# Turning float32-staged pairs of bf16 values as 32-bit words in a matmul, gelu, matmul kernel

## The chip, the cores and the metric

The kernel runs on one core of a Trainium2 chip. The core has five engines that run side by side and meet through semaphores: TensorE (PE: matmuls, and as PEld the loading of their stationary operand), VectorE (DVE), ScalarE (ACT), GpSimd (POOL) and SyncE (SP). TensorE reads SBUF and writes PSUM, which has eight banks of 128 x 512 float32. The metric is the time of one execution in microseconds (us); lower is better.

## The reference

```python
m, k, n, p = 1024, 1024, 2048, 1024      # a: m x k, b: k x n, c: n x p, all float32
h = np.matmul(a, b)
h = 0.5 * h * (1 + np.tanh(np.sqrt(2 / np.pi) * (h + 0.044715 * h ** 3)))
return np.matmul(h, c).astype(np.float32)
```

Two dense products with a gelu (its tanh form) between them.

## The kernel before

All products are made with bf16 or rounded float32 operands. The first product is made transposed: a bank of PSUM holds 128 columns of b by 512 rows of a, so the contraction index k must lie on the partitions for both. b has it there already; a, which is loaded with its rows on the partitions, must be turned. The turned a is the tile `aT`: two halves h of 512 rows each, and for each half eight slices of 128 values of k, 512 columns wide. A quarter q of a is two of these slices, 256 values of k.

The columns of b go through four stretches. The first 512 are made by plain matmuls, `mm1` (line 114), while a and b arrive: four tiles t of 128 columns, two halves h, eight slices k, 64 matmuls of 128x512. This stage is what the change edits. The next 512 columns (`zero`) and then 1024 (`one`) are made by a seven-product scheme (`seven`, its matmuls all on line 212), and so is the whole second product (`two`). The scheme needs sums and differences of quarters of its operands: `t1` to `t4` of the moving side and `s1` to `s4` of the stationary side, made by VectorE (line 170) in float32r, with two plain copies by ScalarE (lines 202 and 208). `BB` names the quarters of `aT` for `zero` and `one`. In `zero` the products run in the order P1, P2, P5, P6, P7, P4, P3; P5 needs s1 and t1, P6 needs s2 and t2, P7 needs s3 and t3, P4 needs t4, P3 needs s4.

The order of all work is written out by hand: each engine runs its instructions in the order of the program text, and semaphores make it wait where data or a buffer is not ready. PSUM banks are named: `bank(i)` gives a new tile in bank i, and the first write to it waits until the tile before it in that bank has been read.

The loads of the first stage go by two queues. From SP (lines 75 to 79) come, in float32, the pieces (0,0), (1,0) and (0,1) of a (half, quarter), and slices 0 to 2 of b's first 512 columns. From POOL (lines 85 to 104) come, converted to bf16 by the DMA, piece (1,1) of a, slice 3 of b, then for q = 2 and 3 the piece (0,q), two slices of b and the piece (1,q); then the next 512 columns of b in two loads of four slices (line 98), the rest of b, and c. A tiny copy (line 81) keeps POOL's loads behind the first piece of a.

The float32 pieces are cast by `cast_a` (VectorE line 110, ScalarE line 108) into a buffer `ab`, the slices of b by `cast_b`. `turn(h, q, i, ab)` is a generator: for each of the two slices of a quarter it emits four transposes of 128x128 bf16 (line 145) into bank i, has VectorE copy the 128x512 result into `aT` (line 146), and yields. The main program (lines 229 to 287) interleaves these steps with blocks of matmuls: `block(h, tiles, ks)` makes the matmuls of one half for some tiles and slices. For q = 1 and 2 it runs four matmuls of half 0, the four transposes of the first slice of (1,q), four matmuls, the transposes of the second slice, then three matmuls of half 1, transposes of (0,q+1), three matmuls, transposes. The fourth tile of half 1 has no bank until half 0 is finished, and is made at the end of the stage, around the turning of (1,3). `stir` emits float32 matmuls on a constant while nothing has arrived.

Of the kernel before, what the change touches and what calls it, by code (L numbers as in the profile page):

```python
# [19 lines left out]
def kernel(ctx, tc, a, b, c, out):  # L20
    nc = tc.nc
    M, K = a.shape
    _, N = b.shape
    _, P = c.shape
    H = 512
    KT = K // 128
# [3 lines left out]
    bv = b.rearrange("(kt p) n -> p kt n", p=128)  # L30
# [3 lines left out]
    consts = ctx.enter_context(tc.tile_pool(name="consts", bufs=1))  # L34
# [5 lines left out]
    def slot(tag, shape, dt, name):  # L40
        return big.tile(shape, dt, name=name, tag=tag)

    def bank(i, shape=(128, H), dt=F32, name="ps"):
        return pp.tile(list(shape), dt, name=name, tag=f"bank{i}", padded_shape=None)

    def pieces(tag, bufs, shape, dt, name):
        return small.tile(shape, dt, name=name, tag=tag, bufs=bufs)

    warm = nc.const_aps.tensor(0.0, [128, 256], F32)
    ident = consts.tile([128, 128], BF16, name="ident")  # L50
    make_identity(nc, ident)
    gate = consts.tile([128, 1], F32, name="gate")
    g = consts.tile([128, 1], F32, name="g")

    consts.tile([128, 16], F32, name="room")

    c_sb = keep.tile([128, NT, P], BF16, name="c_sb")
    hT = [keep.tile([128, NT, H], BF16, name=f"hT{h}") for h in range(2)]
    aT = slot("a", [128, 2, KT, H], BF16, "aT")
    b1 = slot("b1", [128, KT, 1024], BF16, "b1")  # L60
    b2 = slot("b2", [128, KT, 1024], BF16, "b2")


    KH = KT // 2
    stb = slot("x0", [128, KT, H], F32, "stb")
    sta = slot("x1", [128, 2, 2, 4, 256], F32, "sta")
    abq = slot("x3", [128, 4, 2, 4, 256], BF16, "abq")
# [7 lines left out]
    nc.sync.dma_start(out=sta[:, 0, 0], in_=a_part(0, 0))  # L75
    nc.sync.dma_start(out=stb[:, 0:2], in_=b_part(0))  # L76
    nc.sync.dma_start(out=sta[:, 1, 0], in_=a_part(1, 0))
    nc.sync.dma_start(out=sta[:, 0, 1], in_=a_part(0, 1))
    nc.sync.dma_start(out=stb[:, 2], in_=bv[:, 2, 0:H])

    nc.gpsimd.tensor_copy(gate, sta[:, 0, 0, 3, 0:1])
    nc.scalar.activation(g, warm[:, 0:1], AF.Gelu_apprx_tanh)


    def cast_load_a(h, q):
        nc.gpsimd.dma_start(out=abq[:, q, h], in_=a_part(h, q))

    def cast_load_b(q):
        nc.gpsimd.dma_start(out=b1[:, 2 * q:2 * q + 2, 0:H], in_=b_part(q))

    cast_load_a(1, 1)
    nc.gpsimd.dma_start(out=b1[:, 3, 0:H], in_=bv[:, 3, 0:H])
    for q in range(2, 4):
        cast_load_a(0, q)
        cast_load_b(q)
        cast_load_a(1, q)
    for k in range(0, KT, 4):
        nc.gpsimd.dma_start(out=b1[:, k:k + 4, H:], in_=bv[:, k:k + 4, ds(H, H)])
    for n in range(2):
        for k in range(0, KT, 4):  # L100
            nc.gpsimd.dma_start(out=b2[:, k:k + 4, ts(n, H)],
                                in_=bv[:, k:k + 4, ds(1024 + n * H, H)])
# [3 lines left out]
    def copy(eng, dst, src):  # L106
        if eng is nc.scalar:
            nc.scalar.activation(dst, src, AF.Copy)
        else:
            nc.vector.tensor_copy(dst, src)  # L110

    def mm1(p, t, h, ks):
        for k in ks:
            nc.tensor.matmul(p, b1[:, k, ts(t, 128)], aT[:, h, k],  # L114
                             start=(k == 0), stop=(k == KT - 1))

    def gelu(t, h, p):
# [2 lines left out]
    ps = {(0, t): bank(t) for t in range(4)}  # L120

    def stir(*widths):

        for w in widths:
            nc.tensor.matmul(ps[0, 3][:, 0:w], warm[:, 0:128], warm[:, 0:w],
                             start=True, stop=True, skip_group_check=True)

    def cast_a(h, q, *engs):

        ab = pieces("ab", 2, [128, 4, 256], BF16, "ab")  # L130
        for i, eng in enumerate(engs):
            w = 256 // len(engs)
            for j, e in enumerate(eng if isinstance(eng, tuple) else (eng,)):
                m = slice(2 * j, 2 * j + 2) if isinstance(eng, tuple) else slice(0, 4)
                copy(e, ab[:, m, ts(i, w)], sta[:, h, q][:, m, ts(i, w)])
        return ab

    def turn(h, q, i, ab):

        banks = i if isinstance(i, tuple) else (i,)  # L140
        pts = [bank(x, (128, 2, H), BF16, "pt") for x in banks]
        for n in range(2):
            pt = pts[n % len(pts)]
            for m in range(4):
                nc.tensor.transpose(pt[:, n, ts(m, 128)], ab[:, m, ts(n, 128)], ident)  # L145
            nc.vector.tensor_copy(aT[:, h, 2 * q + n], pt[:, n])  # L146
            yield

    def cast_b(k, *engs):
        c0 = 0  # L150
        for i, eng in enumerate(engs):
            w = (H - c0) if i == len(engs) - 1 else H // len(engs) // 128 * 128
            copy(eng, b1[:, k, ds(c0, w)], stb[:, k, ds(c0, w)])
            c0 += w

    def block(h, tiles, ks):
        for k in ks:
            for t in tiles:
# [57 lines left out]
    def pair(i):  # L216
        x = slot(f"x{i}", [128, 2, 4, H], F32R, "x1")
        return x[:, 0], x[:, 1]

    BB = [[aT[:, 0, 0:4], aT[:, 1, 0:4]], [aT[:, 0, 4:8], aT[:, 1, 4:8]]]  # L220
# [9 lines left out]
    tn = turn(0, 0, 4, cast_a(0, 0, nc.vector))  # L230
    next(tn)
    stir(128)
    cast_b(0, nc.vector, nc.vector, nc.scalar)
    next(tn)
    stir(64)
    cast_b(1, nc.scalar)
    ab = cast_a(1, 0, nc.vector, nc.scalar)
    block(0, range(4), (0,))
    block(0, range(2), (1,))
    for _ in turn(1, 0, (7, 6), ab):  # L240
        pass
    block(0, range(2, 4), (1,))
    ab = cast_a(0, 1, (nc.scalar, nc.vector), nc.vector)
    cast_b(2, nc.scalar, nc.scalar)
    for t in range(3):
        ps[1, t] = bank(4 + t)
    zero.t[0], zero.t[1] = pair(2)
    block(1, range(3), (0,))
    tn = turn(0, 1, 7, ab)
    next(tn)  # L250
    block(1, range(3), (1,))
    next(tn)
    zero.t1(4, 0)
    for q in range(1, 3):
        k = 2 * q
        block(0, range(4), (k,))
        tn = turn(1, q, 7, abq[:, q, 1])
        next(tn)
        block(0, range(4), (k + 1,))
# [228 lines left out]
```

## Time and profile before

| | |
|---|---|
| median of 3 runs | 117.55 us (117.53 to 117.62) |
| span of the profiled execution | 115.7 us; its own total time is not given apart from the span |
| PE busy | 111.1 us, 96% of the span |
| DVE, ACT, POOL busy | 90.0, 51.4, 17.2 us |
| granted TensorE clock | 1.00 |
| first matmul of line 114, of line 212 | 6.8 us, 24.29 us |
| HBM read, written | 20.97 MB, 4.19 MB |

The front page gives the span from the first to the last instruction, busy times and the granted clock in 40 slices. The groups give, for each line and shape, the count, the busy time in us and the mean in ns of one, then the idle time of the engine just before them and what ended it. A row of the timeline has the start in us, the time it covers, the engine, the line and operation, the tiles written and read, the shape, how many instructions were merged (x4), and in brackets the idle time before and its releaser. A matmul's duration in the trace holds its drain, which overlaps the next one, so the cost of one in a stream is the distance between starts.

### The profile page before, as it was taken

What the parts mean: (1) busy time and instruction counts of PE and PEld (TensorE: products, weight loads), DVE (VectorE), ACT (ScalarE), POOL (GpSimd) and SP (SyncE); (2) the same over time, 40 slices, a digit from 0 to 9 for tenths busy, and PEclk for the clock granted to TensorE, in tenths of its full rate; (3) what the DMA queues carried; (4) which work ended last, traced back from release to release, by engine and by line L of the source; (5) the groups of instructions that cost most, each with busy time, mean ns of one, the idle gap of its engine ahead of it and who ended that gap; (6) DMA issues with size and microseconds to landing.
All of it is one profiled execution on the core that took longest, in us unless ns stands there. A gap on an engine that the chain in (4) does not pass through costs nothing.

```text
span 115.7 us, 1461 instructions
## 1 busy us (share of the span) xinstructions
PE 111.1 (96%) x542; PEld 77.1 (67%) x542; DVE 90.0 (78%) x107; ACT 51.4 (44%) x86; POOL 17.2 (15%) x29
## 2 busy tenths in 40 slices
PE   7989999999999999999999999999999999999980
PEld 6645555546776447888885444688888888888860
DVE  0347748789999998935699999999999986954770
ACT  5053000999259997166698429500124982000000
POOL 2497755223322000000000000000000000000000
PEclk9999999999999999999999999999999999999999
DMA  2999999999999999998000000060000002014993
GB/s 69 295 381 229 200 199 205 204 208 205 206 211 209 212 213 209 212 210 168 8 0 0 6 0 0 38 235 0 0 0 0 0 4 91 1 73 176 370 363 106
DMA packets 13414, 15.94 MB, mean 138 GB/s; under 512 B 736, under 2 KB 9312, under 8 KB 13408
## 3 DMA queue, kind: packets, MB, share of 16 engines
q0 software_dynamic: 8672, 9.31, 47.6%
q1 hardware_dynamic: 4736, 6.56, 15.8%
q8 instruction: 4, 0.07, 0.3%
q14 instruction: 2, 0.02, 0.0%
HBM read 20.97 MB, written 4.19 MB: 218 GB/s over the span
## 4 chain that ended last, share of the span: by engine, by line
PE 90%; DMA 5%; SPq 1%; DVE 1%; issue 0%
PE ps L212 76%; PE ps L114 11%; DMA sta<-in_a_dram 5%; PE pt L145 3%; SPq L76 0%; DVE ab L110 0%; SPq L75 0%; DVE ot L375 0%
## 5 line engine op out<-in xcount | busy, mean ns | idle before, releaser
L212 PE MATMUL ps<-x,s 128*128 128x512 f32 x128 | 29.6, 391 | 0.0
L212 PEld LDWEIGHTS ps<-x,s 128*128 128x128 f32 x128 | 24.0, 188 | 5.1
L212 PE MATMUL ps<-x,x 128*128 128x512 f32 x96 | 22.9, 394 | 0.0
L212 PEld LDWEIGHTS ps<-x,x 128*128 128x128 f32 x96 | 18.0, 188 | 3.9
L114 PE MATMUL ps<-aT,b 128*128 128x512 bf16 x64 | 16.1, 379 | 0.2 <-DVE b L110 0.2
L298 ACT ACTIVATE v<-ps 128x512 f32<-128x512 f32 x10 | 6.0, 599 | 19.1 <-PE ps L212 19.1
L212 PE MATMUL ps<-c_sb,hT 128*128 128x512 bf16 (+1 forms) x72 | 14.2, 356 | 0.0
L212 PE MATMUL ps<-x 128*128 128x512 f32 x56 | 13.2, 392 | 0.0
L212 PEld LDWEIGHTS ps<-x 128*128 128x128 f32 x56 | 10.2, 188 | 2.6 <-ACT u L298 0.4
L118 ACT ACTIVATE hT<-ps 128x512 bf16<-128x512 f32 x14 | 7.3, 595 | 9.7 <-PE ps L114 9.7
L212 PEld LDWEIGHTS <-hT 128*128 128x128 bf16 x72 | 6.9, 98 | 7.0 <-issue 0.5
L118 ACT ACTIVATE hT<-ot 128x512 bf16<-128x512 f32 x18 | 10.4, 624 | 2.0 <-DVE ot L303 2.0
L212 PE MATMUL ps<-aT,b 128*128 128x512 bf16 x48 | 10.7, 379 | 0.0
L146 DVE COPY aT<-pt 128x512 bf16<-128x512 bf16 x16 | 6.7, 423 | 5.1 <-PE pt L145 5.1
L303 DVE TENSOR_TENSOR ot<-ps,u 128x512 f32<-128x512 f32 x10 | 6.7, 690 | 5.1 <-ACT u L298 5.1
L303 DVE TENSOR_TENSOR ot<-ps,v 128x512 f32<-128x512 f32 x10 | 6.7, 688 | 4.8 <-DMA out_dram<-ot 3.8
L170 DVE TENSOR_TENSOR x<-c_sb 128x1024 fp32r<-128x1024 bf16 x8 | 9.3, 1226 | 0.0
L114 PEld LDWEIGHTS <-b 128*128 128x128 bf16 x64 | 5.7, 98 | 4.5 <-DVE b L110 0.3
L212 PEld LDWEIGHTS <-b 128*128 128x128 bf16 x48 | 4.6, 98 | 5.7 <-issue 0.3
L104 POOL DMA_DIRECT2D c_sb<-in_c_dram x8 | 5.6, 702 | 13.1 <-DMA b<-in_b_dram 12.4
L170 DVE TENSOR_TENSOR x<-b 128x1024 fp32r<-128x1024 bf16 (+1 forms) x4 | 7.0, 1752 | 0.6 <-issue 0.6
L298 ACT ACTIVATE u<-ps 128x512 f32<-128x512 f32 x10 | 5.9, 598 | 3.4 <-PE ps L212 3.2
(44 smaller groups left out, 111.3 us busy)
## 6 DMA issues: line engine op xcount, KB each, us to landing
c_sb<-in_c_dram POOLq DMA_DIRECT2D x8, 512.0 KB, 20.0
out_dram<-ot SPq DMA_DIRECT2D x13, 256.0 KB, 2.1
b<-in_b_dram POOLq DMA_DIRECT2D x6, 512.0 KB, 15.3
sta<-in_a_dram SPq DMA_DIRECT2D x3, 512.0 KB, 6.1
abq<-in_a_dram POOLq DMA_DIRECT2D x5, 256.0 KB, 7.9
out_dram<-ot SPq DMA_DIRECT2D x6, 128.0 KB, 2.0
stb<-in_b_dram SPq DMA_DIRECT2D x1, 512.0 KB, 5.3
b<-in_b_dram POOLq DMA_DIRECT2D x2, 256.0 KB, 8.2
```

The source lines that it names most:

```text
L104: nc.gpsimd.dma_start(out=c_sb[:, t:t + 2], in_=cv[:, t:t + 2])
L114: nc.tensor.matmul(p, b1[:, k, ts(t, 128)], aT[:, h, k], start=(k == 0), stop=(k == KT - 1))
L118: nc.scalar.activation(hT[h][:, t], p, AF.Gelu_apprx_tanh)
L145: nc.tensor.transpose(pt[:, n, ts(m, 128)], ab[:, m, ts(n, 128)], ident)
L146: nc.vector.tensor_copy(aT[:, h, 2 * q + n], pt[:, n])
L170: nc.vector.tensor_tensor(out=dst[:, r], in0=x[:, r], in1=y[:, r], op=op)
L212: nc.tensor.matmul(p[:, ds(c0, w)], l[:, k, ts(j, 128)], r[:, k, ds(c0, w)], start=(start and k == 0), stop=(k == self.kt - 1), skip_group ...
L298: nc.scalar.activation(st, p, AF.Copy)
L303: nc.vector.tensor_tensor(out=ot, in0=p, in1=st, op=ADD)
```

## The change

All of a is staged in float32: the five pieces that came converted from POOL's queue now come unconverted into a second staging tile, and every piece is cast by `cast_a`. The cast writes the two slices of a quarter interleaved: value k of slice 0 and value k of slice 1 stand side by side as one 32-bit word. `turn` takes 128x128 such words as float32, so four transposes, with a float32 identity, turn a whole quarter into one bank of 128x512 words, and one copy brings them into `aT`, whose last dimension is now the pair. Matmuls and the sums read `aT` with a step of two values (the class `Turned` stands for a quarter's slices). `turn` now yields after each transpose, and `block` takes a list of such turns and puts one transpose ahead of each of its matmuls. Each cast but the first is divided by rows between ScalarE (first half) and VectorE. The loads of b's next 512 columns are four of two slices, and parts of `t1`, `t2` and `t3` are emitted later.

```diff
-    ident = consts.tile([128, 128], BF16, name="ident")
+    ident = consts.tile([128, 128], F32, name="ident")
-    aT = slot("a", [128, 2, KT, H], BF16, "aT")
+    aT = slot("a", [128, 2, KT // 2, H, 2], BF16, "aT")
-    sta = slot("x1", [128, 2, 2, 4, 256], F32, "sta")
-    abq = slot("x3", [128, 4, 2, 4, 256], BF16, "abq")
+    sta = [slot(x, [128, 2, 2, 4, 256], F32, "sta") for x in ("x1", "x3")]
...
-    def cast_load_a(h, q):
-        nc.gpsimd.dma_start(out=abq[:, q, h], in_=a_part(h, q))
+    def load_a(h, q):
+        nc.gpsimd.dma_start(out=staged(h, q), in_=a_part(h, q))
...
-    for k in range(0, KT, 4):
-        nc.gpsimd.dma_start(out=b1[:, k:k + 4, H:], in_=bv[:, k:k + 4, ds(H, H)])
+    for k in range(0, KT, 2):
+        nc.gpsimd.dma_start(out=b1[:, k:k + 2, H:], in_=bv[:, k:k + 2, ds(H, H)])
...
-            nc.tensor.matmul(p, b1[:, k, ts(t, 128)], aT[:, h, k],
+            nc.tensor.matmul(p, b1[:, k, ts(t, 128)], aT[:, h, k // 2, :, k % 2],
...
-        ab = pieces("ab", 2, [128, 4, 256], BF16, "ab")
+        ab = pieces("ab", 2, [128, 4, 128, 2], BF16, "ab")
+        w = 4 // len(engs)
         for i, eng in enumerate(engs):
-            w = 256 // len(engs)
-            for j, e in enumerate(eng if isinstance(eng, tuple) else (eng,)):
-                m = slice(2 * j, 2 * j + 2) if isinstance(eng, tuple) else slice(0, 4)
-                copy(e, ab[:, m, ts(i, w)], sta[:, h, q][:, m, ts(i, w)])
+            copy(eng, ab[:, ts(i, w)].rearrange("p m k r -> p m r k"),
+                 staged(h, q)[:, ts(i, w)].rearrange("p m (r k) -> p m r k", r=2))
         return ab
 
     def turn(h, q, i, ab):
 
-        banks = i if isinstance(i, tuple) else (i,)
-        pts = [bank(x, (128, 2, H), BF16, "pt") for x in banks]
-        for n in range(2):
-            pt = pts[n % len(pts)]
-            for m in range(4):
-                nc.tensor.transpose(pt[:, n, ts(m, 128)], ab[:, m, ts(n, 128)], ident)
-            nc.vector.tensor_copy(aT[:, h, 2 * q + n], pt[:, n])
+        pt = bank(i, (128, H), F32, "pt")
+        for m in range(4):
+            nc.tensor.transpose(pt[:, ts(m, 128)], ab[:, m].rearrange("p k r -> p (k r)").bitcast(F32), ident)
+            if m == 3:
+                nc.vector.tensor_copy(aT[:, h, q].rearrange("p m r -> p (m r)").bitcast(F32), pt)
             yield
...
-    def block(h, tiles, ks):
+    def block(h, tiles, ks, turns=()):
+        turns = iter(turns)
         for k in ks:
             for t in tiles:
+                next(turns, None)
                 mm1(ps[h, t], t, h, (k,))
+        for _ in turns:
+            pass
...
-    ab = cast_a(1, 0, nc.vector, nc.scalar)
+    ab = cast_a(1, 0, nc.scalar, nc.vector)
     block(0, range(4), (0,))
-    block(0, range(2), (1,))
-    for _ in turn(1, 0, (7, 6), ab):
-        pass
-    block(0, range(2, 4), (1,))
-    ab = cast_a(0, 1, (nc.scalar, nc.vector), nc.vector)
+    block(0, range(4), (1,), turn(1, 0, 7, ab))
+    ab = cast_a(0, 1, nc.scalar, nc.vector)
...
-    block(1, range(3), (0,))
-    tn = turn(0, 1, 7, ab)
-    next(tn)
+    block(1, range(3), (0,), turn(0, 1, 7, ab))
+    ab = cast_a(1, 1, nc.scalar, nc.vector)
     block(1, range(3), (1,))
-    next(tn)
     zero.t1(4, 0)
     for q in range(1, 3):
         k = 2 * q
-        block(0, range(4), (k,))
-        tn = turn(1, q, 7, abq[:, q, 1])
-        next(tn)
+        block(0, range(4), (k,), turn(1, q, 7, ab))
+        ab = cast_a(0, q + 1, nc.scalar, nc.vector)
         block(0, range(4), (k + 1,))
-        next(tn)
+        block(1, range(3), (k,), turn(0, q + 1, 7, ab))
+        ab = cast_a(1, q + 1, nc.scalar, nc.vector)
+        block(1, range(3), (k + 1,))
         zero.t1(4, q)
-        block(1, range(3), (k,))
-        tn = turn(0, q + 1, 7, abq[:, q + 1, 0])
-        next(tn)
-        block(1, range(3), (k + 1,))
-        next(tn)
-    zero.t1(4, 3)
     block(0, range(4), (6, 7))
-    zero.t2(2, 0)
...
-    mm1(ps[1, 3], 3, 1, range(2))
-    tn = turn(1, 3, 0, abq[:, 3, 1])
-    next(tn)
-    mm1(ps[1, 3], 3, 1, range(2, 5))
-    next(tn)
-    mm1(ps[1, 3], 3, 1, (5,))
+    tn = turn(1, 3, 0, ab)
+    for k in range(4):
+        mm1(ps[1, 3], 3, 1, (k,))
+        next(tn)
+    mm1(ps[1, 3], 3, 1, (4, 5))
+    zero.t1(4, 3)
+    zero.t2(2)
...
-    zero.t3(2, 0)
-    zero.t2(2, 1)
     block(1, range(3), (6, 7))
...
         elif n == "P2":
-            zero.t3(2, 1)
+            zero.t3(2)
```

More of the change, by code (lines that the diff above doesn't have):

```diff
@@ L53 @@
     g = consts.tile([128, 1], F32, name="g")
-    consts.tile([128, 16], F32, name="room")
+    consts.tile([128, 80], F32, name="room")
     c_sb = keep.tile([128, NT, P], BF16, name="c_sb")
     hT = [keep.tile([128, NT, H], BF16, name=f"hT{h}") for h in range(2)]
-    aT = slot("a", [128, 2, KT, H], BF16, "aT")
+    aT = slot("a", [128, 2, KT // 2, H, 2], BF16, "aT")
     b1 = slot("b1", [128, KT, 1024], BF16, "b1")
@@ L73, in b_part, with staged @@
         return bv[:, 2 * q:2 * q + 2, 0:H]
-    nc.sync.dma_start(out=sta[:, 0, 0], in_=a_part(0, 0))
+    def staged(h, q):
+        return sta[q // 2][:, h, q % 2]
+    nc.sync.dma_start(out=staged(0, 0), in_=a_part(0, 0))
     nc.sync.dma_start(out=stb[:, 0:2], in_=b_part(0))
-    nc.sync.dma_start(out=sta[:, 1, 0], in_=a_part(1, 0))
-    nc.sync.dma_start(out=sta[:, 0, 1], in_=a_part(0, 1))
+    nc.sync.dma_start(out=staged(1, 0), in_=a_part(1, 0))
+    nc.sync.dma_start(out=staged(0, 1), in_=a_part(0, 1))
     nc.sync.dma_start(out=stb[:, 2], in_=bv[:, 2, 0:H])
-    nc.gpsimd.tensor_copy(gate, sta[:, 0, 0, 3, 0:1])
+    nc.gpsimd.tensor_copy(gate, staged(0, 0)[:, 3, 0:1])
     nc.scalar.activation(g, warm[:, 0:1], AF.Gelu_apprx_tanh)
-    def cast_load_a(h, q):
-        nc.gpsimd.dma_start(out=abq[:, q, h], in_=a_part(h, q))
+    def load_a(h, q):
+        nc.gpsimd.dma_start(out=staged(h, q), in_=a_part(h, q))
     def cast_load_b(q):
         nc.gpsimd.dma_start(out=b1[:, 2 * q:2 * q + 2, 0:H], in_=b_part(q))
-    cast_load_a(1, 1)
+    load_a(1, 1)
     nc.gpsimd.dma_start(out=b1[:, 3, 0:H], in_=bv[:, 3, 0:H])
     for q in range(2, 4):
-        cast_load_a(0, q)
+        load_a(0, q)
         cast_load_b(q)
-        cast_load_a(1, q)
-    for k in range(0, KT, 4):
-        nc.gpsimd.dma_start(out=b1[:, k:k + 4, H:], in_=bv[:, k:k + 4, ds(H, H)])
+        load_a(1, q)
+    for k in range(0, KT, 2):
+        nc.gpsimd.dma_start(out=b1[:, k:k + 2, H:], in_=bv[:, k:k + 2, ds(H, H)])
     for n in range(2):
@@ L218, in pair, with __init__, __getitem__ @@
         return x[:, 0], x[:, 1]
-    BB = [[aT[:, 0, 0:4], aT[:, 1, 0:4]], [aT[:, 0, 4:8], aT[:, 1, 4:8]]]
+    class Turned:
+        def __init__(self, h, k0):
+            self.h, self.k0 = h, k0
+        def __getitem__(self, at):
+            k = at[1]
+            if isinstance(k, slice):
+                k0, n = self.k0 + k.start, k.stop - k.start
+                q, r = divmod(k0, 2)
+                return aT[:, self.h, q, :, r:r + n].rearrange("p m r -> p r m")
+            q, r = divmod(self.k0 + k, 2)
+            return aT[:, self.h, q, at[2] if len(at) > 2 else slice(0, H), r]
+    BB = [[Turned(0, 0), Turned(1, 0)], [Turned(0, 4), Turned(1, 4)]]
     def quarters(b, c0, w):
@@ L229 @@
     stir(256, 256, 256, 256, 256)
-    tn = turn(0, 0, 4, cast_a(0, 0, nc.vector))
-    next(tn)
-    stir(128)
+    ab = cast_a(0, 0, nc.vector)
+    for n, _ in enumerate(turn(0, 0, 4, ab)):
+        if n == 3:
+            stir(256, 128)
     cast_b(0, nc.vector, nc.vector, nc.scalar)
-    next(tn)
-    stir(64)
     cast_b(1, nc.scalar)
-    ab = cast_a(1, 0, nc.vector, nc.scalar)
+    ab = cast_a(1, 0, nc.scalar, nc.vector)
     block(0, range(4), (0,))
-    block(0, range(2), (1,))
-    for _ in turn(1, 0, (7, 6), ab):
-        pass
-    block(0, range(2, 4), (1,))
-    ab = cast_a(0, 1, (nc.scalar, nc.vector), nc.vector)
+    block(0, range(4), (1,), turn(1, 0, 7, ab))
+    ab = cast_a(0, 1, nc.scalar, nc.vector)
     cast_b(2, nc.scalar, nc.scalar)
@@ L272 @@
     ps[1, 3] = bank(7)
-    mm1(ps[1, 3], 3, 1, range(2))
-    tn = turn(1, 3, 0, abq[:, 3, 1])
-    next(tn)
-    mm1(ps[1, 3], 3, 1, range(2, 5))
-    next(tn)
-    mm1(ps[1, 3], 3, 1, (5,))
+    tn = turn(1, 3, 0, ab)
[5 more added lines that the diff above has]
+    zero.t2(2)
     zero.t[2], x11 = pair(1)
```

## The prediction

> **What bounds the kernel now.** I read the front page first (busy shares, granted clock, the chain that ended last), then the groups kept apart by shape, for prices, then the timeline from 4 to 37 us, where the changed code runs.
>
> ```profile
> span 115.7 us, 1461 instructions
> PE 111.1 (96%) x542; PEld 77.1 (67%) x542; DVE 90.0 (78%) x107; ACT 51.4 (44%) x86; POOL 17.2 (15%) x29
> ...
> PEclk9999999999999999999999999999999999999999
> ...
> PE ps L212 76%; PE ps L114 11%; DMA sta<-in_a_dram 5%; PE pt L145 3%; SPq L76 0%; DVE ab L110 0%; SPq L75 0%; DVE ot L375 0%
> ```
>
> TensorE is the bound: 90% of the chain is its matmuls, at full granted clock, from 6.8 us to the end. So the change is worth exactly what it does to the moment at which TensorE leaves the first stage (lines 114 and 145) and begins the products (line 212, 24.29 us), if nothing behind that moment moves.
>
> ```profile
> L146 DVE COPY aT<-pt 128x512 bf16<-128x512 bf16 x16 | 6.7, 423 | 5.1 <-PE pt L145 5.1
> L434 DVE COPY ot<-ps 128x512 f32<-128x512 f32 x4 | 2.7, 690 | 0.2 <-PE ps L212 0.2
> L108 ACT ACTIVATE ab<-sta 128x512 bf16<-128x512 f32 x1 | 0.6, 629 | 0.4 <-DMA sta<-in_a_dram 0.4
> ```
>
> The prices: an eviction of 512 bf16 columns takes 0.42, one of 512 words 0.69; ScalarE's half of a cast takes 0.63.
>
> ```profile
> 5.38 0.44 PE L125 MATMUL ps<-const-float32-0.0 128*128 128x128 f32 x2
> 7.90 0.43 DVE L110 CAST ab<-sta 128x512 bf16<-128x512 f32 x1 [0.67 <-DMA sta<-in_a_dram]
> 8.38 0.62 PE L145 MATMUL pt<-ident,ab 128*128 128x128 bf16 x8
> ...
> 15.88 0.26 PEld L145 LDWEIGHTS <-abq 128*128 128x128 bf16 x4 [0.28 <-DMA abq<-in_a_dram]
> 15.93 0.39 PE L145 MATMUL pt<-ident,abq 128*128 128x128 bf16 x4
> 16.15 1.03 PE L114 MATMUL ps<-aT,b 128*128 128x512 bf16 x4
> 16.35 0.42 DVE L146 COPY aT<-pt 128x512 bf16<-128x512 bf16 x1 [0.66 <-PE pt L145]
> ...
> 19.07 2.32 PE L114 MATMUL ps<-aT,b 128*128 128x512 bf16 x10
> 21.23 0.39 PE L145 MATMUL pt<-ident,abq 128*128 128x128 bf16 x4
> ...
> 24.29 3.62 PE L212 MATMUL ps<-aT,b 128*128 128x512 bf16 x16
> ...
> 30.53 2.36 DVE L170 TENSOR_TENSOR x<-x,aT 128x1024 fp32r<-128x1024 f32 x2
> 31.42 5.75 PE L212 MATMUL ps<-x 128*128 128x512 f32 x24
> ```
>
> Three things are to be seen. A matmul takes 0.216 (ten from 19.07 to 21.23), a transpose 0.056 (four from 15.93 to 16.15). A copy starts 0.25 after the last transpose of its group starts (16.10 to 16.35), and TensorE follows VectorE by 0.05 (8.33 to 8.38). And the loads of a are nearly in the way already: the piece (half 1, quarter 2) lands at about 15.85, and its transposes start at 15.93.
>
> **The change, part by part.** I write (h,q) for a half and quarter of a, T0 to T3 for its four transposes.
>
> Removed: 32 of 64 transposes, 32 x 0.056 = 1.8 of TensorE; on VectorE 16 copies of 0.42 become 8 of 0.69, 6.7 to 5.5, beside other work. So much is gained.
>
> Added, casts: (1,1), (0,2), (1,2), (0,3), (1,3) were cast by their DMA. Now each costs ScalarE 0.63 and VectorE 0.43 after the landing. ScalarE was idle there for 9.65 us ahead of the first gelu, VectorE has per quarter 2 x 0.69 + 2 x 0.43 + 0.68 = 2.9 of some 3.9 us; the throughput is covered, the latency is not. They write 2-byte values at 4-byte steps, which no row shows: between nothing and the next larger row (ScalarE 128x1024 1.05, so +0.42). I take nothing, the same number of elements.
>
> Added, one handover per four transposes: both slices come free together, and all sit in bank 7. The next turn's T0 and the next matmuls that read the pair wait for T3 + 0.25 + 0.69 + 0.05 = 1.0. Behind a waiting T0 everything on TensorE waits. Before, a half of the work was handed over after 0.25 + 0.42 + 0.05 = 0.72, under three or four matmuls (0.65 or 0.86).
>
> The loads: a now comes unconverted on POOL's queue. The two float32 pieces from SP land 1.43 apart (7.88, 9.31), the converted (1,2) and (0,3) 1.34 apart. I charge 0.07 a piece, 0.2 by the third; bounds nothing and 0.3. The other loads of b1 go in four issues instead of two, 1.5 more of POOL's time; POOL's issues there wait for landings of loads far ahead, so that costs nothing.
>
> The price of a 32-bit transpose: no row has one. Lower bound 0.056. Upper bound: an ordinary float32 matmul of 128 columns, which is two records, 0.44 for both with the tail; four bf16 transposes take 0.39 with a tail and 0.22 without, so 0.27 and some weight loading, say 0.3. I take 0.06, since the moving identity has as many columns as before and each weight load now hides under a 0.216 matmul. The Trainium skill's page "TensorE: Matmul & The Clock Gate" (Terms, xbus) says of its transpose mode that it is four times faster for FP32; against the 0.3 that is an estimate of 0.08 and a sum of about 119.5, which no run here shows yet.
>
> The matmuls on aT now read every second bf16. Lower bound: nothing. Upper: the 24 matmuls with 4-byte operands from 31.42 to 37.01 take 0.233 each, 0.017 more. I take nothing, because part of their excess is waits for ScalarE. The Trainium skill's page "SBUF — State Buffer" (Door 1) speaks for nothing: reads stay at full rate while at least two fall into a 16-byte line, and here four would, 119.3 against 120.7 by the row. No run here shows it yet.
>
> Now the path. (1,0): T0 waits for ScalarE's half, 7.90 + 0.63 + 0.05 = 8.58 (8.38 before, and two matmuls that ran ahead of it are now behind it). Each T with its matmul takes 0.272, so T3 9.40, ready 10.40; only one matmul is between, 0.7 idle. (0,1): T3 11.22, ready 12.22, three matmuls end 11.93, 0.3 idle. (1,1): T3 13.04, ready 14.04, five matmuls end 14.18, no wait. (0,2): T3 15.00, ready 16.00. (1,2): 15.85 + 0.2 for the load, + 0.02 + 0.63 + 0.05 = 16.75: this cast decides, not what went before. From there 36 matmuls 7.78, 12 transposes 0.67, a wait of 1.0 - 0.70 = 0.30 ahead of (0; 6,7), and one of 1.0 - 0.49 = 0.51 ahead of (1; 6,7), since only two matmuls follow T3 of (1,3). Products begin at 26.01, 1.72 later.
>
> Behind it: VectorE cannot begin its subtractions until the copy of (1,3) is done (E), because the last quarter of t1 and both parts of t2 are now queued after it, and the whole of t3 after s2. At the 1.14 pitch of these rows t4 ends at E + 11.1; TensorE begins the products at E + 1.78 and needs t4's second half 9.5 later, at E + 11.25. Covered by 0.1 (0.44 before for the whole of t4); without that cover up to 0.3. The other half of b1 lands at 25.7, ahead of s1. After that TensorE has had no idle time in which a delay could vanish.
>
> Sum: +1.7, so the profile's span goes from 115.7 to 117.4. The execution's own time is its span and what lies around it; its total is not given apart, and the median of the three runs, 117.55, is 1.85 above the span; I keep that and forecast 119.3.
>
> **Rivals.**
> - The 32-bit transpose takes twice the time (0.11). Then (0,2) is ready at 16.84 and decides; 16.84 + 7.78 + 1.32 + 0.80 = 26.74, so 120.0. For it: a 4-byte weight load takes 188 ns here against 98.
> - Strided matmuls pay 0.017: 36 on this path and 48 in the products, 84 x 0.017 = 1.4, so 120.7. For it: all 4-byte rows of line 212 are slower than 0.216. Against it: they differ in the weights, too.
> - The casts slow down with their step: +0.42 at (1,2), 119.7.
> - The change doesn't do what it says, and 32-bit words pass as ordinary float32 matmuls, 0.3 each: T3 of (1,0) at 10.13, (0,2) ready at 19.9, products at 32.1, so 125.3. For it: the constant float32 matmuls do split into two records.
> - The other side: TensorE goes on past a transpose that waits. The waits that I count are 0.9 ahead of 8.58, 0.7, 0.3, 1.0 ahead of 16.75, 0.3 and 0.5, 3.7 in all; once more than 1.7 of them is filled the kernel isn't slower, and with all filled it takes 115.6. Against it: before, the matmuls that stood behind the waiting transposes of (1,0) had their operands by 7.5, and they started only at 8.84, after them.
>
> **How the numbers follow.** My forecast 0.53; doubled transpose 0.13; strided matmuls 0.11; slow casts 0.08; ordinary float32 0.07; the other side 0.05; waits that come out shorter than I count, down to no change, 0.03. The forecast alone spans 119.0 (loads land as before) to 119.6 (the wait at t4 appears). Range 118.5 to 120.9: it takes in the first four cases and leaves out 0.15. Within 0.2% (0.24 us, about what a measurement of this kernel can tell) counts as the same: faster 0.05, same 0.03, slower 0.92.
>
> **What would show it.** In the profile of the changed kernel: transposes 510 instead of 542 records on PE in all (542 if each splits in two); the copy at line 146's place 8 times at about 690; PE idle before a transpose, ended by ScalarE's cast near 8.6 and near 16.7, and by VectorE's copy near 10.4 and 12.2; the first line-212 matmul near 26.0; line-114 matmuls still 0.216 apart. If the products begin at 24.3 or sooner, the waits were wrong; if they begin at 26 and the end is not 1.7 later, the products' stage was.

## The result and the profile after

The changed kernel takes 121.59 us (median of 4 runs, 121.50 to 122.18) against 117.54 (117.39 to 117.62) for the kernel before, run beside it: ratio 1.0358, 95% interval 1.0335 to 1.0382. The forecast was slower, at 119.3 with a range of 118.5 to 120.9. The sign held, the size did not: +4.05 instead of +1.7. The profiled execution took 121.5 in all, its span is 119.7; before it was 115.7. So the 1.8 around the span is what it was, and all of the loss is inside.

From the front page of the changed kernel (busy engines, granted clock, the chain that ended last, the groups with count, busy us, mean ns, then the idle time before and its releaser):

```profile
span 119.7 us, 1412 instructions
...
PE 112.9 (94%) x505; PEld 77.8 (65%) x510; DVE 90.7 (76%) x103; ACT 55.4 (46%) x91; POOL 18.7 (16%) x31
...
PEclk9999999999999999999999999999999999999999
...
PE ps L215 74%; PE ps L116 9%; DMA sta<-in_a_dram 5%; PE pt L143 3%; DVE aT L145 3%; ACT ab L110 1%; SPq L78 0%; SPq L77 0%; DVE ot L378 0%
...
L116 PE MATMUL ps<-aT,b 128*128 128x512 bf16 x62 | 18.0, 388 | 1.1 <-DVE b L112 0.5
...
L145 DVE COPY aT<-pt 128x512 f32<-128x512 f32 x8 | 5.5, 692 | 9.7 <-PE pt L143 9.7
...
L143 PE MATMUL pt<-ident,ab 128*128 128x128 f32 x32 | 8.6, 287 | 1.4 <-DVE aT L145 1.1
...
L110 ACT ACTIVATE ab<-sta 128x512 bf16<-128x512 f32 x7 | 5.5, 780 | 6.9 <-DMA sta<-in_a_dram 5.1
```

The clock is full throughout, so it explains nothing. There are 32 transposes (510 weight loads; five matmul records are missing from this trace) and eight copies of 0.69, as forecast. New in the chain are VectorE's copy (3%, 3.6 us) and ScalarE's cast (1%): TensorE now waits for them. And three prices are not those of the prediction: ScalarE's half of a cast takes 0.78 (0.63 before), a matmul on `aT` 388 ns (379 before, drain included), and the transposes, which only the spacing shows. The timeline of the same kernel (start, time covered, engine, line, tiles, shape, count; in brackets the idle time and its releaser):

```profile
8.70 0.33 PE L143 MATMUL pt<-ident,ab 128*128 128x128 f32 x1 [0.35 <-ACT ab L110]
...
9.43 0.27 PE L143 MATMUL pt<-ident,ab 128*128 128x128 f32 x1
...
9.54 0.39 PE L116 MATMUL ps<-aT,b 128*128 128x512 bf16 x1
...
9.76 0.27 PE L143 MATMUL pt<-ident,ab 128*128 128x128 f32 x1
...
10.07 0.69 DVE L145 COPY aT<-pt 128x512 f32<-128x512 f32 x1 [1.74 <-PE pt L143]
...
10.88 0.14 PEld L143 LDWEIGHTS pt<-ident,ab 128*128 128x128 f32 x1 [1.02 <-ACT b L110]
10.91 0.30 PE L143 MATMUL pt<-ident,ab 128*128 128x128 f32 x1 [0.65 <-DVE aT L145]
...
13.09 0.30 PE L143 MATMUL pt<-ident,ab 128*128 128x128 f32 x1 [0.20 <-DVE aT L145]
...
17.52 0.30 PE L143 MATMUL pt<-ident,ab 128*128 128x128 f32 x1 [0.20 <-DVE aT L145]
...
25.95 1.97 PE L116 MATMUL ps<-aT,b 128*128 128x512 bf16 x8 [0.33 <-DVE aT L145]
27.76 3.78 PE L215 MATMUL ps<-aT,b 128*128 128x512 bf16 x16
```

Read it by starts. A transpose holds TensorE for 9.54 - 9.43 = 0.11 (0.109 to the nanosecond in the trace), not 0.06; the matmul after it for 9.76 - 9.54 = 0.22 (0.226). The copy starts 0.31 after its last transpose and runs 0.69, and TensorE follows at 10.91, 0.15 later: 1.15 from hand to hand. The products begin at 27.76 instead of 24.29: 3.46 of the 4.07 us of span is lost by there. Another 0.60 is lost behind it, 0.48 of it because 48 matmuls on `aT` in the products are 0.010 farther apart, too.

### The profile page after: what moved, and what is told of

Read it like the earlier page. It is cut to its first block, busy times and chain, and to the rows that moved or that the text cites. A ratio compares the mean times of both kernels' runs of the same rounds, so it can differ in the third digit from the quotient of the medians.

```text
span 119.7 us, 1412 instructions
## 1 busy us (share of the span) xinstructions
PE 112.9 (94%) x505; PEld 77.8 (65%) x510; DVE 90.7 (76%) x103; ACT 55.4 (46%) x91; POOL 18.7 (16%) x31
## 4 chain that ended last, share of the span: by engine, by line
PE 86%; DMA 5%; DVE 3%; issue 1%; SPq 1%; ACT 1%
PE ps L215 74%; PE ps L116 9%; DMA sta<-in_a_dram 5%; PE pt L143 3%; DVE aT L145 3%; ACT ab L110 1%; SPq L78 0%; SPq L77 0%; DVE ot L378 0%
## 5 line engine op out<-in xcount | busy, mean ns | idle before, releaser
L116 PE MATMUL ps<-aT,b 128*128 128x512 bf16 x62 | 18.0, 388 | 1.1 <-DVE b L112 0.5
L145 DVE COPY aT<-pt 128x512 f32<-128x512 f32 x8 | 5.5, 692 | 9.7 <-PE pt L143 9.7
L215 PE MATMUL ps<-aT,b 128*128 128x512 bf16 x47 | 11.1, 387 | 0.1
L116 PEld LDWEIGHTS <-b 128*128 128x128 bf16 x64 | 6.3, 98 | 7.0 <-issue 1.0
L143 PE MATMUL pt<-ident,ab 128*128 128x128 f32 x32 | 8.6, 287 | 1.4 <-DVE aT L145 1.1
L110 ACT ACTIVATE ab<-sta 128x512 bf16<-128x512 f32 x7 | 5.5, 780 | 6.9 <-DMA sta<-in_a_dram 5.1
L215 PEld LDWEIGHTS <-b 128*128 128x128 bf16 x48 | 4.5, 96 | 6.3 <-issue 0.3
L112 DVE CAST ab<-sta 128x512 bf16<-128x512 f32 (+1 forms) x8 | 4.1, 511 | 4.9 <-DMA sta<-in_a_dram 4.9
```

Of the source, the lines that this page charges most:

```text
L116: nc.tensor.matmul(p, b1[:, k, ts(t, 128)], aT[:, h, k // 2, :, k % 2], start=(k == 0), stop=(k == KT - 1))
L143: nc.tensor.transpose(pt[:, ts(m, 128)], ab[:, m].rearrange("p k r -> p (k r)").bitcast(F32), ident)
L145: nc.vector.tensor_copy(aT[:, h, q].rearrange("p m r -> p (m r)").bitcast(F32), pt)
L215: nc.tensor.matmul(p[:, ds(c0, w)], l[:, k, ts(j, 128)], r[:, k, ds(c0, w)], start=(start and k == 0), stop=(k == self.kt - 1), skip_group ...
```

## Experiments

Every kernel ran beside the kernel before on its chip. The table has medians and the difference between the two; the changed kernel itself stands at +4.05. "First product" is the start of the first matmul of the products in the profiled execution. Names that begin with b start from the kernel before, those with a from the changed one. The two with one time have no interval.

| run | us | before | difference | ratio (95% interval) | first product |
|---|---|---|---|---|---|
| before | 117.54 | | | | 24.29 |
| after | 121.59 | 117.54 | +4.05 | 1.0358 (1.0335 to 1.0382) | 27.76 |
| b_step2_products | 118.02 | 117.49 | +0.53 | 1.0056 (1.0029 to 1.0083) | 24.36 |
| a_dense_reads | 120.83 | 117.49 | +3.34 | 1.0295 (1.0268 to 1.0322) | 28.04 |
| a_f32r_turn | 120.32 | 117.49 | +2.83 | one time | 26.58 |
| b_float_staging | 118.13 | 117.49 | +0.64 | 1.0052 (1.0037 to 1.0067) | 24.77 |
| a_copy_twice | 126.41 | 117.60 | +8.81 | one time | 32.69 |
| a_two_ahead | 119.91 | 117.60 | +2.31 | 1.0196 (1.0172 to 1.0220) | 25.94 |
| a_vector_first | 121.19 | 117.60 | +3.59 | 1.0305 (1.0285 to 1.0325) | 27.55 |
| a_dense_cast | 121.30 | 117.60 | +3.70 | 1.0313 (1.0293 to 1.0333) | 27.50 |
| a_four_undone | 119.12 | 117.53 | +1.59 | 1.0129 (1.0089 to 1.0169) | 25.66 |
| a_turn_later | 118.72 | 117.54 | +1.18 | 1.0073 (1.0039 to 1.0107) | 25.24 |
| b_three_first | 117.71 | 117.53 | +0.18 | 1.0011 (0.9987 to 1.0036) | 24.53 |
| b_three_split | 117.69 | 117.53 | +0.16 | 1.0004 (0.9988 to 1.0021) | 24.74 |

**Does the step of two values slow a matmul?** First in the kernel before, where nothing else changes:

```diff
+            turned = any(r is x for row in BB for x in row)
...
-                nc.tensor.matmul(p[:, ds(c0, w)], l[:, k, ts(j, 128)], r[:, k, ds(c0, w)],
+                rk = r[:, k, ds(c0, w)]
+                if turned:
+                    rk = r[:, k // 2 * 2:k // 2 * 2 + 2].rearrange("p r m -> p (r m)").rearrange("p (m s) -> p m s", s=2)[:, :, k % 2]
+                nc.tensor.matmul(p[:, ds(c0, w)], l[:, k, ts(j, 128)], rk,
```

> The kernel before, with one thing of the change alone: the 48 bf16 matmuls of zero and one that read aT take every second value out of two neighbouring slices instead of 512 values in a row (so these products see mixed slices; the amount of work is the same). Theory 'step': reading with a step of two costs 0.010 a matmul, 226 ns from start to start where they were 216, 48 x 0.010 = 0.49, so 118.0 (117.9 to 118.1). Rival 'company': the 226 ns seen after the change come from something else beside them; then they stay at 216 ns and the time at 117.5.

The groups of this kernel, the stage's matmuls first, then those of the products:

```profile
L114 PE MATMUL ps<-aT,b 128*128 128x512 bf16 x64 | 16.3, 379 | 0.3 <-DVE b L110 0.3
...
L216 PE MATMUL ps<-aT,b 128*128 128x512 bf16 x48 | 11.2, 387 | 0.0
```

Same type, same shape, same weights; only the step differs, and 379 becomes 387 (216 to 226 ns from start to start). 48 x 0.010 = 0.48 of the +0.53. Then the counterpart, the changed kernel with all 112 matmuls on `aT` reading in a row:

```diff
-            nc.tensor.matmul(p, b1[:, k, ts(t, 128)], aT[:, h, k // 2, :, k % 2],
+            nc.tensor.matmul(p, b1[:, k, ts(t, 128)], aT[:, h, k // 2].rearrange("p m r -> p (m r)")[:, ds(k % 2 * H, H)],
...
-            return aT[:, self.h, q, at[2] if len(at) > 2 else slice(0, H), r]
+            return aT[:, self.h, q].rearrange("p m r -> p (m r)")[:, ds(r * H, H)]
```

> The changed kernel, whose 112 matmuls on aT read 512 values in a row of each quarter's words instead of every second one (so they see mixed slices; all else is as in the changed kernel). Theory 'step': 216 ns again; the 64 of the first stage give 0.65, of which the waits for the copies take some 0.2 back because the matmuls that cover them are shorter, the 48 of the products 0.49, together 0.95, so 120.6 (120.4 to 120.8). Rival 'company': 226 ns stay, 121.6.

The matmuls are 216 ns apart everywhere again, and the excess falls from 4.05 to 3.34, by 0.71 where 0.95 was expected. Its profiled execution (121.45, the longest of its four) can't say where the rest went by absolute times, since there piece (1,0) of a landed at 8.6 instead of 7.85. Counted from the first transpose of (1,0), it has 18.60 to the products where the changed kernel has 19.06, 0.46 less. Behind the start of the products it has 91.64 instead of 91.98, only 0.34 less where 0.49 was expected, because a wait appears there that the changed kernel does not have. At 39.00 a weight load of the products starts after 0.32 of waiting for VectorE's first addition into `ot` (line 306), which stands behind VectorE's sums in its order, and two matmuls start 0.28 and 0.34 apart instead of 0.23. That is 0.16 lost: TensorE comes sooner, VectorE does not. So 0.46 and 0.34, 0.80 in all, stand against 0.71 in the medians. The price of the step is shown; what it is worth in time depends on what else is ready.

**What does a 32-bit transpose cost, and is it the type or the word?** float32r words of the same size in place of float32 (its casts write half the elements, 128 of each 256):

```diff
+    ident_r = consts.tile([128, 128], F32R, name="ident_r")
+    nc.vector.tensor_copy(ident_r, ident)
...
-        ab = pieces("ab", 2, [128, 4, 128, 2], BF16, "ab")
+        ab = pieces("ab", 2, [128, 4, 128], F32R, "ab")
...
-            copy(eng, ab[:, ts(i, w)].rearrange("p m k r -> p m r k"),
-                 staged(h, q)[:, ts(i, w)].rearrange("p m (r k) -> p m r k", r=2))
+            copy(eng, ab[:, ts(i, w)], staged(h, q)[:, ts(i, w), 0:128])
...
-        pt = bank(i, (128, H), F32, "pt")
+        pt = bank(i, (128, H), F32R, "pt")
...
-            nc.tensor.transpose(pt[:, ts(m, 128)], ab[:, m].rearrange("p k r -> p (k r)").bitcast(F32), ident)
+            nc.tensor.transpose(pt[:, ts(m, 128)], ab[:, m], ident_r)
...
```

> The changed kernel with its transposes in float32r instead of float32. The words turned are rounded float32 values of one slice, not pairs, and each cast makes half as many elements; so only the distance from a transpose to the matmul behind it is compared, not the time. Theory 'columns': a float32 word takes TensorE two cycles per moving column, 128 x 2 at the clock of these rows is 107 ns, which is all of the 108 ns seen; a float32r one takes one, so 55 to 60 ns. Rival 'fixed': the price is that of a 4-byte weight load or of changing between 4-byte and 2-byte work, and 108 ns stay. The time would be about 119.7 by the first and 121.1 by the second.

Three neighbours in its timeline, PE alone:

```profile
9.27 0.40 PE L118 MATMUL ps<-aT,b 128*128 128x512 bf16 x1
...
9.31 0.42 PE L145 MATMUL pt<-ident_r,ab 128*128 128x128 f32 x1
...
9.57 0.40 PE L118 MATMUL ps<-aT,b 128*128 128x512 bf16 x1
```

The split between the two is modelled oddly here (0.26 and 0.04), but a pair is 9.57 - 9.27 = 0.30, against 9.76 - 9.43 = 0.33 in the changed kernel and 0.272 before. To the nanosecond the pairs take 301, 335 and 272, so with 226, 226 and 216 for the matmul a transpose takes 75 (float32r), 109 (float32) and 56 (bf16). Neither named value was met: of the 53 ns that float32 takes more than bf16, some 34 go with float32, and some 19 stay with float32r. What makes these parts is open. What matters here is that one float32 word costs as much as two bf16 values: behind the first piece 28 x 0.109 = 3.05 stand against 56 x 0.056 = 3.14, so halving the count gained nothing.

**What does staging in float32 cost by itself?** The kernel before with float32 pieces and engine casts, but bf16 transposes, so that every piece is converted as in the changed kernel and written in a row:

```diff
-    abq = slot("x3", [128, 4, 2, 4, 256], BF16, "abq")
+    sta = [slot(x, [128, 2, 2, 4, 256], F32, "sta") for x in ("x1", "x3")]
...
-        nc.gpsimd.dma_start(out=abq[:, q, h], in_=a_part(h, q))
+        nc.gpsimd.dma_start(out=staged(h, q), in_=a_part(h, q))
...
-        tn = turn(1, q, 7, abq[:, q, 1])
+        tn = turn(1, q, 7, ab)
         next(tn)
         block(0, range(4), (k + 1,))
+        ab = cast_a(0, q + 1, nc.scalar, nc.vector)
...
```

> The kernel before, with only the staging of the change: all of a comes unconverted, and ScalarE and VectorE cast the pieces (1,1), (0,2), (1,2), (0,3), (1,3), slice by slice; transposes, copies and matmuls as before. Theory 'four prices': the staging alone puts a cast of 0.63 between the landing of (1,2) and its transposes, 15.7 + 0.63 + 0.1 = 16.4 against 15.93, and some waits on VectorE's queue: 0.3 to 0.8 more, 117.9 to 118.4. Rival 'staging': the casts are the main loss; then 2 or more, 119.5 and up.

+0.64, with the products at 24.77 (+0.48), and the transposes of (1,2) start at 16.41 where 16.4 was expected; what they wait for last is VectorE's copy of the turn before, which stands behind its half of the cast. So the longer way from landing to transpose is worth about a sixth of the loss. A cast of 128x512 written in a row takes ScalarE 0.63 here, on the same data. To see whether the step of its output explains the 0.78, the changed kernel with casts written in a row (the words then pair other values):

```diff
-        ab = pieces("ab", 2, [128, 4, 128, 2], BF16, "ab")
+        ab = pieces("ab", 2, [128, 4, 2, 128], BF16, "ab")
...
-            copy(eng, ab[:, ts(i, w)].rearrange("p m k r -> p m r k"),
+            copy(eng, ab[:, ts(i, w)],
...
-            nc.tensor.transpose(pt[:, ts(m, 128)], ab[:, m].rearrange("p k r -> p (k r)").bitcast(F32), ident)
+            nc.tensor.transpose(pt[:, ts(m, 128)], ab[:, m].rearrange("p r k -> p (r k)").bitcast(F32), ident)
```

> The changed kernel, with its casts writing their values in a row (so a word holds two neighbours of one slice, and the result differs; the shapes and counts of all instructions stay). Theory 'step': ScalarE's half goes from 0.78 to 0.63, since the 4-byte step of its 2-byte writes costs it 0.29 ns an element, and VectorE's stays at 0.45; the first transpose of (1,0) comes 0.15 sooner: 121.45. Rival 'dims': ScalarE is slower because the cast walks three dimensions instead of two; then 0.78 and 121.6 stay.

Its group of ScalarE's casts:

```profile
L110 ACT ACTIVATE ab<-sta 128x512 bf16<-128x512 f32 x7 | 4.4, 631 | 7.7 <-DMA sta<-in_a_dram 7.7
```

780 becomes 631: the form of the write is the cause. Two things of the form change together here, the step of two values and the number of dimensions that the write walks (three, 2 x 2 x 128, become one of 512), so the rival 'dims' is not excluded. Against it: the casts of the kernel before write rows of 128, two dimensions without a step, and take 0.63. The excess falls by 0.35 where 0.15 was expected for T0 of (1,0), the one place where this cast decides. In the profile the products come 0.25 sooner, and 0.13 of that is an earlier landing of (1,0) in that execution (7.74 for the cast's start instead of 7.87), so the cast itself is worth some 0.12 to 0.14 there. The next kernel removes the same wait in another way, by giving VectorE, which takes 0.46, the rows that are turned first:

```diff
-    ab = cast_a(1, 0, nc.scalar, nc.vector)
+    ab = cast_a(1, 0, nc.vector, nc.scalar)
```

> The changed kernel, with one cast turned round: for the piece (1,0) VectorE has the first half of the rows and ScalarE the second. Theory 'four prices': the first transpose of (1,0) waits for ScalarE's 0.78 after the landing; VectorE's half takes 0.46, so it starts 0.3 sooner, and since nothing up to (1,2) waits for a load, the whole stage moves by 0.3: 121.3 (121.15 to 121.4). Rival 'anchor': a later wait for a load or a cast (the piece (1,2)) takes it back, and the time stays at 121.6.

T0 of (1,0) starts at 8.47 instead of 8.70, though (1,0) landed 0.09 later, and the products come 0.20 sooner; in the medians the excess falls by 0.46. In both runs what is won at this first wait arrives at the products nearly whole (0.25 of 0.27, 0.20 of 0.23): nothing behind it absorbs it.

**Is the handover the path?** The same copy made twice:

```diff
             if m == 3:
-                nc.vector.tensor_copy(aT[:, h, q].rearrange("p m r -> p (m r)").bitcast(F32), pt)
+                for _ in range(2):
+                    nc.vector.tensor_copy(aT[:, h, q].rearrange("p m r -> p (m r)").bitcast(F32), pt)
```

> The changed kernel with each copy from PSUM made twice. Theory 'handover': VectorE's second copy adds 0.6 to each handover; five turns have no cover left and two have some 0.1: (1,0), (0,1), (0,2), (0,3), (1,3) by 0.6, (1,1) and (1,2) by 0.5, the first matmul's delay is swallowed by the wait for the cast of (1,0): 4.0 more in all, 125.5 (124.5 to 126). Rival 'casts' or 'transposes': the copy is not on the path, and less than 1 is added.

Its timeline at the first of these handovers:

```profile
10.05 1.42 DVE L146 COPY aT<-pt 128x512 f32<-128x512 f32 x2 [1.74 <-PE pt L143]
...
11.61 0.30 PE L143 MATMUL pt<-ident,ab 128*128 128x128 f32 x1 [1.38 <-DVE aT L146]
```

TensorE waits 1.38 instead of 0.65: the added 0.73 is paid in full. The products come 4.93 later, nearly the seven times 0.73 = 5.1 that all handovers behind the first piece could cost, so almost every one of them is on the path. The expectation of +4.0 was low by 0.8, outside its range: the second copy takes 0.73, not 0.6.

The other way round, two transposes ahead of each of the first two matmuls of a block, so that the last one comes sooner and more matmuls are left to cover the handover:

```diff
                 next(turns, None)
+                next(turns, None)
                 mm1(ps[h, t], t, h, (k,))
...
-    for k in range(4):
-        mm1(ps[1, 3], 3, 1, (k,))
-        next(tn)
-    mm1(ps[1, 3], 3, 1, (4, 5))
+    for k in range(2):
+        mm1(ps[1, 3], 3, 1, (k,))
+        next(tn)
+        next(tn)
+    mm1(ps[1, 3], 3, 1, (2, 3, 4, 5))
```

> The changed kernel with two transposes ahead of each of the first two matmuls of a block instead of one ahead of each of four. Theory 'handover': the waits after each turn are 1.15 (0.31 from T3 to the copy, 0.69 copy, 0.15 to the next T0) less the matmuls that follow T3; with T3 two matmuls sooner five waits of 0.81, 0.36, 0.36, 0.27 and 0.49 shrink by up to 0.45 each, 1.8 in all, and the pairs of transposes back to back pay their weight load, some 0.06 for each of 14 pairs: 1.0 less, 120.6 (120.2 to 121.0). Rival 'casts': TensorE really waits for the casts behind; then nothing is won, 121.6 to 122.4.

```profile
8.58 0.44 PE L143 MATMUL pt<-ident,ab 128*128 128x128 f32 x2 [0.30 <-ACT ab L110]
...
9.08 0.38 PE L143 MATMUL pt<-ident,ab 128*128 128x128 f32 x2
...
9.30 0.84 PE L116 MATMUL ps<-aT,b 128*128 128x512 bf16 x3
9.50 0.69 DVE L145 COPY aT<-pt 128x512 f32<-128x512 f32 x1 [1.29 <-PE pt L143]
...
10.34 0.41 PE L143 MATMUL pt<-ident,ab 128*128 128x128 f32 x2 [0.20 <-DVE aT L145]
```

In this timeline of the kernel with two ahead, the copy starts 9.50 - 8.58 = 0.92 after the first transpose of (1,0) instead of 1.37, three matmuls run under it instead of one, and the wait on it falls from 0.65 to 0.20. The excess falls by 1.74, more than the 1.0 expected. In the profile the products come 1.81 sooner, 0.12 of it by an earlier landing, which leaves 1.69. Two transposes in a row are 0.109 apart (9.30 - 9.08 = 0.22 for two), so in such a pair their 0.14 weight loads are hidden even without a matmul between them, and the 0.06 charged for each pair did not appear. This is the largest single part of the loss: it lies in where the turns stand, which the longer handover makes dear.

**Do the parts add up?** Four of these edits together (two ahead, VectorE first, casts in a row, reads in a row):

> The changed kernel with four of its prices taken away together: two transposes ahead of a matmul, VectorE first for the piece (1,0), casts that write in a row, matmuls that read in a row (so words and slices are mixed and the result differs; the amount of work stays). What is left of the change is the staging in float32, the copy of 0.69 per turn, and 28 transposes at 0.109 in place of 56 at 0.056, which is the same 3.1. Theory 'four prices': from 119.9 the first cast gives 0.35, the dense reads 0.49 in the products and 0.4 in the stage: 118.6 (118.3 to 118.9), close to the 118.1 of the kernel before with float32 staging alone. Rival 'something else': a price not found yet keeps it above 119.2.

It missed by 0.5. The timeline of that kernel shows the place:

```profile
15.72 0.63 ACT L110 ACTIVATE ab<-sta 128x512 bf16<-128x512 f32 x1 [1.90 <-DMA sta<-in_a_dram]
...
16.40 0.44 PE L143 MATMUL pt<-ident,ab 128*128 128x128 f32 x2 [0.32 <-ACT ab L110]
```

With everything ahead of it faster, the cast of (1,2) decides, as the prediction had said of the plain change, and TensorE stands idle ahead of it with four ready matmuls behind the waiting transpose. Another 0.15 of the miss lies in the products, where the wait for VectorE's addition appears as in a_dense_reads (91.66 behind their start, 92.01 with two ahead alone). The first reading was put to a run: the turn of this piece goes ahead of the third and fourth matmul.

```diff
-    def block(h, tiles, ks, turns=()):
+    def block(h, tiles, ks, turns=(), skip=0):
...
-                next(turns, None)
-                next(turns, None)
+                for _ in range(2 if skip <= 0 else 0):
+                    next(turns, None)
+                skip -= 1
                 mm1(ps[h, t], t, h, (k,))
...
-        block(0, range(4), (k,), turn(1, q, 7, ab))
+        block(0, range(4), (k,), turn(1, q, 7, ab), 2 * (q == 2))
```

> The kernel of a_four_undone, with one thing moved: the turn of (1,2) stands ahead of the third and fourth matmul of its block of four (half 0, slice 4), no longer ahead of the first and second. The theory says that a_four_undone missed its number because the cast of (1,2) decided there: TensorE had nothing in front of it, came to T0 0.48 too early, and had all four matmuls of that block still to do behind the turn. Two of them moved in front fill 0.43 of that wait: T0 of (1,2) stays at 16.40, the first matmul of the products comes at 25.23 in place of 25.66, and the time is 118.7 (118.55 to 118.85), still over the kernel before. The rival: something other than the order there holds TensorE (the handover ahead of the next block, or the loads), then the wait moves on to the matmuls of slice 5 or to the turn behind, the products begin at 25.6, and the time stays at 119.1 (119.0 to 119.2).

```profile
14.85 1.67 PE L116 MATMUL ps<-aT,b 128*128 128x512 bf16 x7
...
16.42 0.44 PE L143 MATMUL pt<-ident,ab 128*128 128x128 f32 x2
```

Seven matmuls run ahead of the transpose instead of five, the wait is gone from the brackets, the transpose still starts at 16.42, the products begin at 25.24 for 25.23 expected, and the time is 118.72 for 118.7. What is left over the kernel before is +1.18. In the profile 0.49 of it is this transpose (15.93 before: there the DMA had already converted the piece), 0.43 the two matmuls that stand behind it instead of ahead, and 0.25 lies behind the start of the products, 0.16 of it that wait again. This kernel reads values in a row that are not the ones the product needs, so it is a measurement, no version to use.

**Can the kernel before gain from the same idea?** It has two matmuls of slice 1 ahead of the transposes of (1,0), and TensorE then waits for the cast; a third can go there:

```diff
-    block(0, range(2), (1,))
+    block(0, range(3), (1,))
     for _ in turn(1, 0, (7, 6), ab):
         pass
-    block(0, range(2, 4), (1,))
+    block(0, range(3, 4), (1,))
```

> The kernel before, with three instead of two matmuls ahead of the transposes of (1,0), where TensorE is idle for 0.25 until the cast is done. Theory 'anchor': the transposes of (1,2) start as their load lands (15.9), so what is won ahead of it is waited for there: 117.5 (117.4 to 117.6). Rival 'free': 0.2 less, 117.3.

And with that, the load of b's slices 4 and 5 split in two, so that (1,2) of a is issued between them:

```diff
-        cast_load_b(q)
-        cast_load_a(1, q)
+        if q == 2:
+            nc.gpsimd.dma_start(out=b1[:, 4, 0:H], in_=bv[:, 4, 0:H])
+            cast_load_a(1, q)
+            nc.gpsimd.dma_start(out=b1[:, 5, 0:H], in_=bv[:, 5, 0:H])
+        else:
+            cast_load_b(q)
+            cast_load_a(1, q)
```

> As the run with three matmuls first, and the load of slices 4 and 5 of b is split, with the piece (1,2) of a between them, so that it lands some 0.65 sooner and slice 5 no sooner than the block that needs it. Theory 'anchor': with the landing out of the way the 0.2 come through: 117.3 (117.2 to 117.4). Rival: slice 5 becomes the anchor, or another load; 117.5 or more.

Neither differs from the kernel before by more than its interval. The first was expected so by the theory 'anchor', but not for the reason that the theory gives. In its profile:

```profile
8.98 0.76 DVE L146 COPY aT<-pt 128x512 bf16<-128x512 bf16 x2 [0.64 <-PE pt L145]
9.00 1.26 PE L114 MATMUL ps<-aT,b 128*128 128x512 bf16 x4
```

Four matmuls cover 1.26, what five cover in the kernel before: behind the first of them TensorE waits 0.24, because the other three belong to half 1 and need the turned (1,0), whose first copy ends at 9.40. The first matmul of half 1 starts at 9.46, 0.90 after T0 of (1,0); in the kernel before that distance is 0.91, and in the second run 0.91 again. So the matmul that went ahead of the transposes is missing behind them, and the handover of (1,0) takes back at once what was won. The landing of (1,2) does not decide: in the first run its transposes start at 16.16, straight behind a matmul and 0.23 after the landing; in the second the piece lands at 15.37, and its transposes start at 16.37 all the same. The anchor theory is refuted: that the first run gains nothing was forecast by luck. No version here beats the kernel before.

## Why the prediction was right in sign and wrong in size

**Right.** That TensorE's arrival at the products is what counts: 3.46 of 4.07 came before it, and most of the rest (0.48 of 0.60) was a price paid at every matmul, not a wait. The 0.70 ahead of T0 of (0,1) and the 0.30 ahead of (1,1) were forecast; 0.81 and 0.36 came (starts compared; the brackets, which count the modelled drain, show 0.65 and 0.20). No wait ahead of (0,2), and 0.30 and 0.51 ahead of the two last blocks, which came as 0.27 and 0.49. The cover at t4 held: the changed kernel has no new wait at that point of the products. The other side, TensorE passing a waiting transpose, did not occur: the copy made twice was paid for at once.

**Wrong: "Removed: 32 of 64 transposes, 32 x 0.056 = 1.8" with "I take 0.06".** A transpose measured 0.109, in the lower quarter of the bounds 0.056 to 0.3, and just the rival of the doubled transpose. So 32 of them cost 3.5 where 64 had cost 3.6, and the 1.8 was not gained. The reason given, as many columns as before, does not carry: with the same 128 columns bf16 takes 0.056, float32r 0.075 and float32 0.109. The Trainium skill's page "TensorE: Matmul & The Clock Gate" (Terms, xbus) says that transpose mode is four times faster for FP32; the estimate of 0.08 from it was nearer than the 0.06 taken, but the trace does not reach it, at 0.109.

**Wrong: strided matmuls, "I take nothing".** They take 0.010 more, inside the bounds of nothing and 0.017, 112 times. The Trainium skill's page "SBUF — State Buffer" (Door 1), which speaks of full rate while at least two reads fall into a 16-byte line, disagrees with the rows: four fall into one here, and 216 became 226.

**Wrong: the cast, "I take nothing, the same number of elements".** 0.15 of a bound of 0.42, by the form of the write alone.

**Wrong: the handover "T3 + 0.25 + 0.69 + 0.05 = 1.0".** It is 0.31 + 0.69 + 0.15 = 1.15. The 0.25 and the 0.05 were measured on bf16: the first contains the tail of a transpose, which is longer for a float32 one (0.27 against 0.22 in the rows), and the 0.05 came from a bf16 transpose. The trace shows where the 0.15 goes: the weight load of T0 waits for the copy too. The copy ends at 10.76, the load starts at 10.88, and the transpose follows at 10.91. With bf16 transposes (b_float_staging) the load of (1,2) has started at 16.26, ahead of the copy's end at 16.35, and the transpose starts at 16.41. A plain matmul behind such a copy follows after 0.05 in the changed kernel too (21.80 to 21.85). Why the float32 load waits was not tested.

**Wrong in consequence: "16.75: this cast decides, not what went before".** The loads came no later than before (the cast of (1,2) starts at 15.79, so the 0.2 charged did not appear), and the cast ended at 16.57. But what went before was only through at 17.52. Of that 0.77, the path from T0 of (1,0), forecast to reach the same point at 16.00, is late by 1.52: 0.12 at its start, 4 x 3 x 0.064 = 0.77 for transposes with their matmuls, 3 x 0.15 = 0.45 for the handovers that bind ((1,0), (0,1), (0,2)), and 0.18 of smaller things, five matmuls at 0.010 among them. From T0 of (1,2) to the products there are 12 x 0.053 = 0.64 for transposes and 36 x 0.010 = 0.36 for matmuls, less 0.05 for two waits that came out shorter, 0.95 of the 0.98 by which 10.24 is more than 9.26. So 1.72 + 0.77 + 0.98 = 3.47 against 3.46 measured, and 0.60 more behind the start of the products.

**A harmless miss:** the first matmul came at 7.27, not unchanged at 6.83. It waits for VectorE's two casts of b, which in this execution took 0.50 and 0.44 instead of 0.23 and 0.22, behind a copy that ended at 6.80. It need not be so: a_vector_first, whose program is the same up to there, began at 6.88. Why the casts took longer is open. TensorE still reached T0 of (1,0) 0.5 before the cast did, so it cost nothing.

**The method's fault:** doubled transpose, strided matmuls and slow casts each stood as a rival with a time of its own, 120.0, 120.7 and 119.7, as if one of them at most could be true. All three were true in part at once, and they add up on one path. A range whose upper end is the worst single rival leaves out every pair of them. And a handover longer than 1.0 stood among the rivals not at all.

## What to carry to other kernels

Before narrow operations are merged into fewer wide ones, measure one wide operation between its real neighbours: a float32 transpose here cost as much as two bf16 ones, and the pairs then bought nothing for a step of two paid by 112 matmuls. On an engine that runs in order, a turn that is handed over through another engine wants its transposes close together, as early as their data allow and no earlier, with ready matmuls in front of a late one and enough of them behind it: that order alone was worth 1.7 of the 4.05 here. Unknown prices on one path are to be added, not set against each other.

## What the runs showed of the hardware

- A matmul of 512 bf16 columns takes 226 instead of 216 ns when its moving operand is read with a step of 4 bytes, in both kernels and with full clock.
- A 128x128 transpose costs TensorE 56 ns in bf16, 75 in float32r, 109 in float32, beside matmuls; in float32 also in pairs back to back, with weight loads of 140 ns (98 in bf16) hidden.
- Behind VectorE's copy from PSUM a float32 transpose that waits for it starts 0.145 us after the copy's end, its weight load 0.11 after; a bf16 transpose or a plain matmul starts 0.05 after.
- ScalarE needs 0.78 instead of 0.63 us for 128x512 float32 to bf16 when it writes 2-byte values at 4-byte steps in three dimensions (which of the two does it was not separated); VectorE mostly 0.45 instead of 0.42 (0.42 in the run with casts in a row).
- Unconverted loads of a, twice the bytes into SBUF, landed no later than the converted ones: the piece (1,2) at 15.68 instead of 15.84.
